# The modulation's weight loads stand in pairs in the load stream of a hybrid decoder layer

## The chip, the cores and the metric

One core of a Trainium2 chip runs the whole kernel. Times are device microseconds of that core; the kernel before took 1602.75 us as the median of three runs (1599.96 to 1604.44). Its profile is one further execution.

## The reference, cut to what matters

One inference step of one decoder layer, for a prompt of 256 tokens and eight sequences with one new token each, with the same weights. The conditioning vectors `c` (1 + 8 rows) give the modulation; the rest of the layer needs it at two places.

```python
mod = silu(c) @ w_mod + b_mod                    # (9, 2048) @ (2048, 6144)
shift, scale, gate = split(mod, 3)
h = rmsnorm(x, g_pre) * (1 + scale) + shift      # needed by every product with w_in
(u, v, z, xb, zb, q, k, v, qi, ki, wi, zc, gm) = split(h @ w_in)
...                                              # three branches: gMLP, RG-LRU, sparse attention
o = merged @ w_out
y = x + gate * rmsnorm(o, g_post)                # gate is needed at the end only
```

All of it is float32.

## The kernel before, in words

**Weights.** All 264 columns (256 prompt tokens and 8 samples) stay in SBUF; the weights stream past. A weight tile (a "w item") is one load of 512 KB from `in_wall`: eight blocks of 128x128. ScalarE rounds it to a high part (`wh`, L157 through `split_high`), VectorE makes the low part (`wl`, L160 through `split_low`), in two halves of 512 columns each, and TensorE multiplies each block three times (high x high, high x low, low x high: L1008 in `product`). So a w item is 24 products of 264 columns in fp32r. There are 482 of them, numbered from 0 in the order of the stream.

**Modulation.** An "m item" is one load of 512 KB from `in_wmod`, which TensorE reads as it is, in fp32, with the conditioning (`cpad`, padded to 32 columns) as the stationary operand (L394 in `mod_item`). The result of each takes only 32 columns of the array, and up to four groups lie side by side in the tile `pmod`: the profile shows these products with a tile of 128*32, those of L1008 with 128*128. An item of 1024 columns is 4 products, 8 in the profile, since it shows two for each fp32 product. There are 96 m items. The hidden state is built in six pieces of 1, 1, 2, 4, 4, 4 blocks of 128 features (`PIECES`); piece q needs the items m q.0, m q.1 and so on: 4, 4, 8, 16, 16 and 16 of them. The last 32, m 6.x and m 7.x, make the gate.

**The order of the work** is a list, `STREAM`, written out by `_stream` (L75 to L98) before anything is emitted. It sets the order of the loads on SP's queue, of the splits and of the products alike. It begins with the 4 items of piece 0. Then come the first 32 output blocks (`EARLY`), one piece of features at a time: the w items of piece q, with the m items of piece q + 1 between them, each as soon as its due position has come (`MOD_BY`, L83). That is 4, 4, 8, 16, 16 and 16 w items, w0 to w63. Then come the other blocks whole, two w items each; in the part of `u` and `za` (the gMLP branch) one gate item follows every w item until the 32 gate items are used up (L90 to L95).

**Buffers.** Loads land in ten buffers, six called `raw` and four called `rawx`; after the last item of piece 5 only the six are left (`room`, L243). They are taken from a list in the order in which they were given back (`load`, L248; `used`, L259). An m item gives its buffer back when TensorE has read it; a w item when VectorE has made the second half of `wl`. A load waits on SP until its buffer is free, and every load behind it waits with it. The split tiles `wh` and `wl` have three buffers each (`AHEAD + 1`): a tile is split two tiles ahead of its products in the main part, one ahead at the beginning (`split_plan`, L270). The work of ScalarE and VectorE is emitted in the order of the list too: a split that stands before the evacuations of a tile (`part`, L159 and L1014) holds them up while it waits.

**Index keys.** When the last item of piece 5 has been emitted, `gather_kix` (L473) puts 32 small loads (L483) on SP's queue. They come behind the weight loads that had been emitted by then, and ahead of all the others.

```python
    for i, it in enumerate(items):
        while room(loaded):
            load(loaded); loaded += 1
        ...
            split_plan(); split_some(...)
        if it[0] == "m":
            mod_item(i); continue
        ...                                  # a w item: product() for its blocks
```

Of the kernel before, what the change touches and what calls it, by code (L numbers as in the profile page):

```python
# [36 lines left out]
ORDER = [("ki", 0)]  # L37
# [37 lines left out]
def _stream():  # L75


    items, n = [("m", 0, i) for i in range(len(MODS[0]))], 0
    for q, (k0, nk) in enumerate(PIECES):
        ms = [("m", q + 1, i) for i in range(len(MODS[q + 1]))] if q + 1 < len(PIECES) else []  # L80
        done = 0
        for j in range(0, EARLY, 8 // nk):
            while done < len(ms) and done * MOD_BY <= j * len(ms):  # L83
                items.append(ms[done])
                done += 1
            items.append(("w", n, [(x, k0, nk) for x in range(j, j + 8 // nk)]))
            n += 1
        assert done == len(ms)
    gate = [("m", q, i) for q in range(len(PIECES), len(MODS)) for i in range(len(MODS[q]))]
    for j in range(EARLY, len(ORDER)):  # L90
        for k0 in (0, 8):
            items.append(("w", n, [(j, k0, 8)]))
            n += 1
            if gate and ORDER[j][0] in ("u", "za"):
                items.append(gate.pop(0))  # L95
    return items


STREAM = _stream()


# [1084 lines left out]
```

## Time and profile before

| | us |
|---|---|
| median of three runs | 1602.75 (1599.96 to 1604.44) |
| the profiled execution, its own time | 1604.95 |
| its span, first to last instruction | 1603.2 |
| TensorE busy | 1572.6 |
| VectorE busy | 987.1 |
| ScalarE busy | 808.1 |
| mean granted TensorE clock | 0.993 |

The span runs from the first to the last instruction of the core. Busy products overlap, so the distance between the starts of two products is what one costs, not its own duration. In the rows PE is TensorE's product, PEld its weight load, DVE VectorE, ACT ScalarE, POOL GpSimd, SPq the queue of SyncE. L394 means line 394 of the kernel. An entry in brackets gives the idle time of the engine just before the row and what ended it.

### The profile page before, as it was taken

The page shows a single profiled execution, that of the slowest core. Times are in us where ns is not written, and L with a number is a line of the kernel's source. Part 1 is how long each engine was busy: PE and PEld are TensorE (multiplying, and loading weights), DVE is VectorE, ACT ScalarE, POOL GpSimd, SP SyncE. Part 2 cuts the span into 40 slices and gives each one's busy share as a digit, 9 for nine tenths or more (in the row PEclk, how much of TensorE's full clock was granted, in tenths as well). Part 3 has the DMA queues.
Part 4 walks back from the last instruction along what each step waited for, and adds up shares of the span by engine and source line. Part 5 has one row for each costly group of instructions (what it writes and reads, how often), then busy time and mean ns, then how long its engine had stood idle before and what let it go on. Part 6 is the DMA issues. An engine that isn't in the chain of part 4 may idle for free.

```text
span 1603.2 us, 33544 instructions
## 1 busy us (share of the span) xinstructions
PE 1572.6 (98%) x13353; PEld 1517.7 (95%) x13353; DVE 987.1 (62%) x2100; ACT 808.1 (50%) x1628; POOL 148.0 (9%) x255
## 2 busy tenths in 40 slices
PE   8999979999999999999999999999999999999998
PEld 7888878999999999998889999999999999999998
DVE  6776558865566546444456654444777777766554
ACT  5333337755555444443334444444777777744442
POOL 4000007300000001000000000000211211100011
PEclk9999989999999999999999999999999999999999
DMA  8898753666555656557875556555455555555652
GB/s 337 306 344 290 272 186 114 197 211 195 158 172 170 197 179 197 187 190 265 285 278 174 177 185 228 185 184 180 156 192 172 172 169 187 172 190 185 236 182 84
DMA packets 99773, 326.28 MB, mean 204 GB/s; under 512 B 11552, under 2 KB 23200, under 8 KB 99232
## 3 DMA queue, kind: packets, MB, share of 16 engines
q1 hardware_dynamic: 98816, 322.98, 59.7%
q8 instruction: 105, 1.72, 0.4%
q10 hardware_dynamic: 800, 1.15, 0.2%
q14 instruction: 52, 0.43, 0.1%
HBM read 320.35 MB, written 3.67 MB: 202 GB/s over the span
## 4 chain that ended last, share of the span: by engine, by line
PE 91%; DVE 3%; DMA 2%; ACT 1%; SPq 1%; issue 1%; DVEq 0%; ACTq 0%
PE acc L1008 85%; PE pmod L394 2%; DMA raw<-in_wall 2%; DVE wl L160 1%; SPq L483 1%; ACT wh L157 1%; PE spP L836 0%; PE sP L668 0%; PE oP L680 0%; DMA xr<-in_xT 0%; PE giP L877 0%; PE gaP L877 0%; DVE part L159 0%; PE soP L744 0%; PE ssP L718 0%
## 5 line engine op out<-in xcount | busy, mean ns | idle before, releaser
L160 DVE TENSOR_TENSOR wl<-raw,wh 128x512 fp32r<-128x512 f32 x926 | 612.6, 706 | 387.3 <-ACT wh L157 380.2
L1008 PE MATMUL acc<-hh,wh 128*128 128x264 f32 x2832 | 822.1, 290 | 7.4 <-DVE part L159 3.3
L1008 PE MATMUL acc<-hh,wl 128*128 128x264 f32 x2832 | 805.1, 284 | 1.9 <-DVE wl L160 1.9
L1008 PE MATMUL acc<-hl,wh 128*128 128x264 f32 x2832 | 805.8, 285 | 0.1
L157 ACT ACTIVATE wh<-raw 128x512 fp32r<-128x512 f32 x926 | 530.3, 622 | 498.7 <-PE acc L1008 319.8
L1008 PEld LDWEIGHTS acc<-hh,wh 128*128 128x128 f32 x2832 | 536.1, 189 | 39.4 <-issue 26.1
L1008 PEld LDWEIGHTS acc<-hl,wh 128*128 128x128 f32 x2832 | 536.6, 189 | 0.7 <-DVE hl L160 0.4
L1008 PEld LDWEIGHTS acc<-hh,wl 128*128 128x128 f32 x2832 | 534.0, 189 | 2.3 <-DVE wl L160 2.3
L1008 PE MATMUL acc<-ah,wh 128*128 128x264 f32 x768 | 217.9, 284 | 0.0
L1008 PE MATMUL acc<-al,wh 128*128 128x264 f32 x768 | 217.6, 283 | 0.0
L1008 PE MATMUL acc<-ah,wl 128*128 128x264 f32 x768 | 217.5, 283 | 0.0
L1008 PEld LDWEIGHTS acc<-al,wh 128*128 128x128 f32 x768 | 144.8, 188 | 0.0
L1008 PEld LDWEIGHTS acc<-ah,wh 128*128 128x128 f32 x768 | 144.7, 188 | 0.0
L1008 PEld LDWEIGHTS acc<-ah,wl 128*128 128x128 f32 x768 | 144.0, 187 | 0.0
L159 DVE TENSOR_TENSOR part<-acc,part 128x264 f32<-128x264 f32 x128 | 51.8, 427 | 37.6 <-PE acc L1008 37.2
L1008 PE MATMUL acc<-mh,wh 128*128 128x264 f32 x256 | 72.6, 284 | 0.0
L1008 PE MATMUL acc<-ml,wh 128*128 128x264 f32 x256 | 72.5, 283 | 0.0
L1008 PE MATMUL acc<-mh,wl 128*128 128x264 f32 x256 | 72.5, 283 | 0.0
L808 POOL TENSOR_TENSOR mg<-mg,gp 128x264 f32<-128x264 f32 x16 | 12.1, 753 | 473.3 <-DMA raw<-in_wall 310.7
L1008 PEld LDWEIGHTS acc<-ml,wh 128*128 128x128 f32 x256 | 48.2, 188 | 0.0
L1008 PEld LDWEIGHTS acc<-mh,wh 128*128 128x128 f32 x256 | 48.2, 188 | 0.0
L1008 PEld LDWEIGHTS acc<-mh,wl 128*128 128x128 f32 x256 | 48.0, 187 | 0.0
(362 smaller groups left out, 1142.2 us busy)
## 6 DMA issues: line engine op xcount, KB each, us to landing
raw<-in_wall SPq DMA_DIRECT2D x463, 512.0 KB, 3.6
raw<-in_wmod SPq DMA_DIRECT2D x73, 512.0 KB, 4.7
rawx<-in_wmod SPq DMA_DIRECT2D x23, 512.0 KB, 6.2
rawx<-in_wall SPq DMA_DIRECT2D x19, 512.0 KB, 5.6
gk<-in_ck SPq DMA_DIRECT2D x32, 128.0 KB, 3.5
gv<-in_cv SPq DMA_DIRECT2D x32, 128.0 KB, 4.1
xr<-in_xT SPq DMA_DIRECT2D x4, 528.0 KB, 6.3
wrg<-in_wrg SPq DMA_DIRECT2D x1, 2048.0 KB, 9.9
```

The costliest lines, as they stand in the source:

```text
L157: copy = lambda out, x, scale=1.0: act.activation(out, x, AF.Copy, scale=scale)
L159: add = lambda out, x, y: dve.tensor_tensor(out, x, y, OP.add)
L160: sub = lambda out, x, y: dve.tensor_tensor(out, x, y, OP.subtract)
L394: pe.matmul(MOD[q][32 * g:32 * g + 32, 0:n], cpad[:, k, :], r[:, c:c + n], start=k == 0, stop=k == KB - 1, skip_group_check=True)
L483: sp.dma_start(kix[h:h + 64, b, g * P:(g + 1) * P], a["cidx"][bass.ds(S["pages"][i] * 64, 64), :])
L808: pool.tensor_tensor(S["mg"][:, j, :], S["mg"][:, j, :], x, OP.add)
L1008: pe.matmul(c[:, 0:T], x[:, kk * P:(kk + 1) * P], y[:, k, :], start=n == 0 and (kk == 0 if early else k == 0), stop=n == 2 and (kk == nk - ...
```

## The change

Two loops of `_stream` put m items into the list two at a time. In the early part, when the next m item is due, it and the one after it are appended together. In the part of `u` and `za`, two gate items follow the second w item of a block instead of one following each. Number, content and mutual order of the m items stay; so do those of the w items. What else follows, follows from the new order: which buffer a load gets, and what stands ahead of it in each queue.

```diff
@@ _stream, early part @@
             while done < len(ms) and done * MOD_BY <= j * len(ms):
-                items.append(ms[done])
-                done += 1
+                items += ms[done:done + 2]
+                done += 2
             items.append(("w", n, [(x, k0, nk) for x in range(j, j + 8 // nk)]))
             n += 1
@@ _stream, the other blocks @@
         for k0 in (0, 8):
             items.append(("w", n, [(j, k0, 8)]))
             n += 1
-            if gate and ORDER[j][0] in ("u", "za"):
-                items.append(gate.pop(0))
+        if gate and ORDER[j][0] in ("u", "za"):
+            items += gate[:2]
+            del gate[:2]
```

The list between w7 and w15, before and after (an m item as piece.number):

```
before  3.0 w8 3.1 3.2 w9 3.3 3.4 3.5 w10 3.6 3.7 3.8 w11 3.9 3.10 3.11 w12 3.12 3.13 3.14 w13 3.15 w14 w15
after   3.0 3.1 w8 3.2 3.3 w9 3.4 3.5 w10 3.6 3.7 3.8 3.9 w11 3.10 3.11 w12 3.12 3.13 3.14 3.15 w13 w14 w15
```

At the very beginning it was `0.0 0.1 0.2 0.3 1.0 w0 1.1 w1 1.2 w2 1.3 w3` and becomes `0.0 0.1 0.2 0.3 1.0 1.1 w0 w1 1.2 1.3 w2 w3`.

## Rows read from the trace of the kernel before

**Rows 1.** The page, part 1: busy us, share of the span, instructions

```profile
PE 1572.6 (98%) x13353; PEld 1517.7 (95%) x13353; DVE 987.1 (62%) x2100; ACT 808.1 (50%) x1628; POOL 148.0 (9%) x255
```

**Rows 2.** The page, part 4: the chain of waits by line

```profile
PE acc L1008 85%; PE pmod L394 2%; DMA raw<-in_wall 2%; DVE wl L160 1%; SPq L483 1%; ACT wh L157 1%; PE spP L836 0%; PE sP L668 0%; PE oP L680 0%; DMA xr<-in_xT 0%; PE giP L877 0%; PE gaP L877 0%; DVE part L159 0%; PE soP L744 0%; PE ssP L718 0%
```

**Rows 3.** Stretch of the gates: length, busy PE PEld DVE ACT POOL, clock, DMA share, GB/s

```profile
714.60:832.06 117.46, 117.46 (x1028) 100.44 (x1027) 57.23 (x109) 44.34 (x86) 0.00 (x0) 1.00 0.79 276
```

**Rows 4.** Timeline of PE around one gate item: start us, us, what

```profile
714.48 0.28 PE L1008 MATMUL acc<-hl,wh 128*128 128x264 f32 x1
714.60 0.28 PE L1008 MATMUL acc<-hh,wl 128*128 128x264 f32 x1
714.81 0.64 PE L394 MATMUL pmod<-raw,cpad 128*32 128x256 f32 x8
...
715.61 0.28 PE L1008 MATMUL acc<-hl,wh 128*128 128x264 f32 x1
```

**Rows 5.** Timeline of PE around two m items in a row, piece 4

```profile
109.28 0.28 PE L1008 MATMUL acc<-hh,wl 128*128 128x264 f32 x1
109.49 0.64 PE L394 MATMUL pmod<-rawx,cpad 128*32 128x256 f32 x8
109.95 0.61 PE L394 MATMUL pmod<-raw,cpad 128*32 128x256 f32 x8
...
110.72 0.29 PE L1008 MATMUL acc<-hl,wh 128*128 128x264 f32 x1
```

**Rows 6.** Timeline of ACT and of DVE: one split in the gates

```profile
734.09 1.15 ACT L157 ACTIVATE wh<-raw 128x512 fp32r<-128x512 f32 x2 [2.72 <-DMA raw<-in_wall]
...
734.75 1.29 DVE L160 TENSOR_TENSOR wl<-raw,wh 128x512 fp32r<-128x512 f32 x2 [2.58 <-ACT wh L157]
```

**Rows 7.** The page, part 6: loads, KB each, median us from issue to landing

```profile
raw<-in_wall SPq DMA_DIRECT2D x463, 512.0 KB, 3.6
```

**Rows 8.** Timeline of SP's queue: the index-key loads: start us, us, what

```profile
199.07 22.36 SPq L483 DMA_DIRECT2D kix<-in_cidx  x32
```

**Rows 9.** Timeline of SP's queue: the issues of w11, w12 and w13

```profile
65.19 0.42 SPq L257 DMA_DIRECT2D raw<-in_wall  x1
...
72.65 0.33 SPq L257 DMA_DIRECT2D raw<-in_wall  x1
...
79.85 0.33 SPq L257 DMA_DIRECT2D raw<-in_wall  x1
```

**Rows 10.** Timeline of SP's queue: the issues of w0 and of m1.1

```profile
9.36 0.33 SPq L257 DMA_DIRECT2D raw<-in_wall  x1
10.66 0.33 SPq L255 DMA_DIRECT2D rawx<-in_wmod  x1
```

**Rows 11.** Timeline of ACT: the split of w0

```profile
19.77 1.15 ACT L157 ACTIVATE wh<-raw 128x512 fp32r<-128x512 f32 x2 [1.57 <-DMA raw<-in_wall]
```

**Rows 12.** Timeline of ACT: the splits of w11, w12 and w13

```profile
70.67 1.16 ACT L157 ACTIVATE wh<-raw 128x512 fp32r<-128x512 f32 x2 [4.76 <-PE pmod L394]
77.87 1.15 ACT L157 ACTIVATE wh<-raw 128x512 fp32r<-128x512 f32 x2 [6.05 <-DMA raw<-in_wall]
84.48 1.15 ACT L157 ACTIVATE wh<-raw 128x512 fp32r<-128x512 f32 x2 [5.45 <-DMA raw<-in_wall]
```

**Rows 13.** Timeline of PE: the first product of w13, and the item behind it

```profile
86.92 0.36 PE L1008 MATMUL acc<-hh,wh 128*128 128x264 f32 x1 [1.89 <-DVE part L159]
...
91.52 0.64 PE L394 MATMUL pmod<-raw,cpad 128*32 128x256 f32 x8
```

**Rows 14.** Stretch after PE's wait at w13, columns as in rows 3

```profile
88.00:90.00 2.00, 2.00 (x12) 2.00 (x11) 1.67 (x4) 1.32 (x3) 0.00 (x0) 0.52 0.96 377
```

**Rows 15.** Second half of the opening, columns as in rows 3

```profile
60.00:98.36 38.36, 35.59 (x331) 29.65 (x329) 26.02 (x67) 12.73 (x26) 0.00 (x0) 0.96 0.93 351
```

**Rows 16.** DMA, 0 to 100 us: what the engines moved in 40 equal slices

```profile
GB/s 30 177 355 412 412 404 406 410 405 406 407 410 367 244 208 329 187 318 69 347 167 410 264 313 408 418 310 360 365 259 362 357 211 377 288 331 379 405 415 410
```

## The prediction, made before the changed kernel was run

> **What bounds the kernel now.** The busy times come first: PE is busy 1572.6 of 1603.2 us [rows 1]. A busy PE alone proves little, so the chain of waits is read next: 85% of it is the trunk's product (L1008), 2% the modulation's product (L394), and 1% each is work that PE waits for, among it the loads of the index keys on SP's queue, L483 [rows 2]. Then the stretches: from 714.60 to 832.06, where the 32 gate loads are consumed, PE is busy for the whole 117.46 us at full clock [rows 3]. There every nanosecond saved on PE is saved at the end. Only two places are not PE's, and the sum takes them up: the opening up to about 92 us, where weights and their splitting come late, and the loads of the index keys.
>
> **The count.** The change is said to halve 96 changes of tile width to 48. Walking the list by its rule says otherwise, since neighbours already shared a visit. Runs of m items before, then after: head with piece 1, 4 then 2; piece 2, 4 then 4; piece 3, 7 then 6; pieces 4 and 5, 12 then 8 each; gates, 32 then 16. That is 71 then 44: 27 visits go, not 48.
>
> **The price of one visit.** PE's timeline shows one m item alone: the last product of a weight tile starts at 714.60, the second product after the item at 715.61, 1.01 us [rows 4]. I count to the second product because the first after an item is slow as well. Two plain steps of 0.12 (714.48 to 714.60) would have taken 0.24, so a lone item costs 0.77. With two items in a row the same distance is 109.28 to 110.72, 1.44 us, less 0.24: 1.20 [rows 5]. The second item costs 0.43. A merged visit therefore saves 0.77 - 0.43 = **0.34 us**; as both kinds run in the kernel of before, this price needs no guess.
>
> **The sum, part by part.**
> - Gates: 16 merges in a stretch where PE never idles [rows 3]: 16 x 0.34 = -5.4 us. All of it reaches the end if loads keep up. After the change every other weight load goes into a buffer that the splitting of the tile two ahead sets free. That splitting takes 1.95 us (ACT from 734.09, DVE to 736.04) [rows 6]. From there four tiles of 24 x 0.12 = 2.9 us and two pairs of 1.2, less the 1.95 already gone, leave 12.0 us before the product, 10.0 before the tile's own splitting must begin. A load takes 3.6 [rows 7]. Covered.
> - Pieces 4 and 5: 8 merges, but the last of them (the end of piece 5) lies after the point from which the index-key loads are timed, so its 0.34 is lost in that wait: 7 x 0.34 = -2.4.
> - Index-key loads: SP works in order. They start at 199.07 and hold the queue for 22.36 us before the next weights [rows 8]. Before, two weight loads stand behind the last splitting that frees a buffer ahead of them; after, only one does, the other having got its buffer from PE earlier. One issue of 0.42 [rows 9] fewer: -0.4. Gathering is called one tile earlier, but with one more tile already loaded, so PE runs dry at the same tile.
> - The start pays. Loads go out in stream order, and m1.1 now stands before tile 0. Tile 0's load is issued at 9.36, the next at 10.66 [rows 10]; ACT sat waiting for it until 19.77 [rows 11]. One place later is **+1.3**. The bounds are 0, if later waits of this stage swallow it, and +3, if PE's longer idling also brings a further stretch at half clock, priced below. I take 1.3, which the two rows give.
> - The wait at tile 13 goes. Tiles 11, 12 and 13 use one buffer in turn, so each load waits for the splitting of the tile before: issued at 65.19, 72.65, 79.85 [rows 9], while ACT gets them at 70.67, 77.87 and 84.48 [rows 12]. PE then idles 1.89 us before 86.92, and the tile that begins there takes 4.6 us to the next item (91.52) instead of 2.9 [rows 13]: the granted clock is 0.52 in that stretch, the lower level of 1.2 GHz, after that idling [rows 14]. By the changed list tile 12 gets the buffer of m3.3, which PE frees before tile 9, and goes out behind the splitting of tile 10, not 11. What limits it then is the queue, which in the full opening issues a load per 1.3 us [rows 10]: tile 11, behind one more m item, lands near 71.9, then m3.10, m3.11 and tile 12 at 75.8, 2.0 sooner than 77.87. Its splitting (1.95) ends near 77.8; m3.15 and tile 13 go out behind it, at 78.3; with the same 4.6 to landing (79.85 to 84.48) tile 13 is there at 82.9 and split at 84.9. PE arrives at 85.0 as before plus one item of 0.43, so it no longer waits and does not idle its clock away: 1.9 and 1.7, **-3.6**. Bounds: 0, if landing takes longer as loads come sooner, and -4.
> - Nothing else is added: instructions, bytes and loads are the same, and the m items move earlier, so what they compute is ready no later.
>
> Sum: -5.4 - 2.4 - 0.4 + 1.3 - 3.6 = -10.5 us. The profiled execution took 1604.95 (span 1603.2 and 1.75 around it), which gives 1594.45. It lies 2.2 above the median of the runs, 1602.75; against that the forecast is 1602.75 - 10.5 = 1592.25, rounded **1592.5**.
>
> **Rivals.**
> - *The opening is bound by bytes.* From 60 to 98.36 us the queue moved 351 GB/s, its share 0.93 [rows 15]; if that is the ceiling, no order of loads brings tile 13 sooner, the wait stays, and the start's 1.3 may stay too: -5.4 - 2.4 - 0.4 + 1.3 = -6.9, or 1595.9. Against it: the same queue moved 404 to 412 GB/s over several slices between 7.5 and 30 us, and later fell as low as 69 [rows 16]. There is room. The Trainium skill (DMA: Bandwidth & Descriptors, Specifications) limits one core's HBM reads to about 358 GB/s, which would make this rival the likeliest. By that rule the trace disagrees with its 412. Chance 0.22.
> - *It does what it says.* 48 visits vanish: 48 x 0.34 = -16.3, or 1586.4. The walk of the list speaks against it; it could come near only if the opening also gained more than I see. Chance 0.05.
> - *No change.* PE reaches its tiles sooner and waits there for loads, so the gates give nothing: -2.4 - 0.4 + 1.3 is -1.5, or 1601.3. For it: in bursts a pair asks for three loads at once. Against it: the 12.0 us of lead. Chance 0.12.
> - *Slower: loads late at the gates.* With pairs, two buffers of six hold m tiles at the same time, and every other weight load starts only after a splitting. It decides once a load takes over 10.0 us instead of 3.6. To lose 4.8 net after gaining 10.5, 16 such tiles must each be late by 15.3 / 16 = 0.96 us, so loads would take about 11 us: 1607.6. The gate stretch runs its DMA at 0.79 share and 276 GB/s [rows 3], far from the 412 that this queue has shown. Chance 0.06.
>
> **How the numbers follow.** The forecast has 0.55. Its own spread is the opening's terms and the clock after the index-key loads, where PE restarts at half clock for a stretch whose end may shift by a couple of us. The range, 1586 to 1600, holds these, the rival of bytes and the one of 48; no change and slower (0.18 together) are left out. A measurement of this kernel can tell about 0.3%, 4.8 us, so faster means below 1597.9. Faster is the forecast (0.55), two thirds of the rival of bytes (0.15 of 0.22), whose middle lies only 2 us below that bound, and the one of 48 (0.05): 0.75. Within 0.3% is the rest of the bytes (0.07) and the third rival (0.12): 0.19. Slower 0.06.
>
> **What would show it.** PE's timeline in the gates: pairs with 1.44 us between the products around them, weight tiles of 2.9 us, and no wait named between; the stretch of the gates shorter by 5.4. In the opening: tile 0's load landing near 21, no idle time of PE near 87 us and no granted clock below 1 there. The index-key loads should start near 194 (199.07 + 1.3 - 3.6 - 2.4 - 0.4). Wrong it would be if a pair cost twice 0.77, if ACT in the gates waited for loads with PE idle behind it, or if PE still idled before tile 13.

## The result, and the profile after

The changed kernel takes 1612.89 us, the median of five runs (1610.25 to 1614.11); the kernel before ran five times beside it with a median of 1602.3 (1599.96 to 1604.44). The ratio is 1.0062, with an interval of 1.0051 to 1.0073: about 10 us slower. Forecast were 1592.5 us, with 1586 to 1600 as the range, so even the sign was wrong. The profiled execution took 1614.11 us (span 1612.3). All line numbers behind the edit are one higher than before, and L395, L1009, L158 and L161 are the L394, L1008, L157 and L160 of the rows above.

Parts 1 and 4 of the profile's page of the changed kernel (busy time; the chain that ended last):

```profile
PE 1572.5 (98%) x13353; PEld 1523.6 (94%) x13353; DVE 985.8 (61%) x2100; ACT 806.7 (50%) x1628; POOL 148.4 (9%) x255
...
PE acc L1009 82%; DMA raw<-in_wall 3%; PE pmod L395 2%; DVE wl L161 2%; DMA rawx<-in_wall 1%; SPq L484 1%; ACT wh L158 1%; DVE part L160 1%; DMA xr<-in_xT 0%; PE sP L669 0%; PE oP L681 0%; PE spP L837 0%; PE giP L878 0%; PE gaP L878 0%; PE soP L745 0%
```

The number of instructions is that of [rows 1], and so, to 0.1 us, is PE's busy time. The chain is where the difference shows: the trunk's product fell from 85% to 82% [rows 2], and what came in its place are loads (3% and 1%) and splits. PE waits more, and for weights.

Where along the kernel it does so is read by counting products: 24 of them make a weight tile, so the start of every tile can be found on PE's timeline in both traces. After minus before, in us:

| tile | w0 | w12 | w13 | w16 | w48 | w52 | w192 | w200 | w206 | w210 | w214 | w222 | w230 | w480 |
|---|---|---|---|---|---|---|---|---|---|---|---|---|---|---|
| | +1.25 | -0.01 | +2.19 | +3.18 | -0.04 | -0.54 | -0.73 | -1.74 | -2.75 | -3.30 | -0.77 | +4.79 | +9.16 | +9.20 |

From tile 194 the gate items come. Up to tile 210 each pair brings about its 0.34 us, as forecast (2.57 us in eight). Then, in twenty tiles, more than 12 us are lost, and nothing changes behind. The stretch of the gates, with the same columns as [rows 3], is:

```profile
714.00:841.50 127.50, 117.82 (x1039) 103.29 (x1037) 54.24 (x104) 42.16 (x85) 0.00 (x0) 0.99 0.66 240
```

PE stands still for 9.7 of 127.5 us, where [rows 3] had none, and the DMA moves less per second, 240 GB/s instead of 276. The pair itself costs what it should. PE's timeline around one of them, early in the gates:

```profile
738.65 0.28 PE L1009 MATMUL acc<-hh,wl 128*128 128x264 f32 x1
738.86 1.07 PE L395 MATMUL pmod<-raw,cpad 128*32 128x256 f32 x16
739.86 0.39 PE L1009 MATMUL acc<-hh,wh 128*128 128x264 f32 x1
740.09 0.28 PE L1009 MATMUL acc<-hl,wh 128*128 128x264 f32 x1
```

From 738.65 to 740.09 are 1.44 us, the very figure of [rows 5]. What PE waits for stands on SP's queue, ACT and PE a little later. SP's queue (start, us, what):

```profile
762.01 0.80 SPq L256 DMA_DIRECT2D raw<-in_wmod  x2
762.87 2.59 SPq L258 DMA_DIRECT2D raw<-in_wall  x2
770.17 0.80 SPq L256 DMA_DIRECT2D raw<-in_wmod  x2
771.02 0.90 SPq L258 DMA_DIRECT2D raw<-in_wall  x2
779.63 0.80 SPq L256 DMA_DIRECT2D raw<-in_wmod  x2
780.49 2.58 SPq L258 DMA_DIRECT2D raw<-in_wall  x2
788.03 0.80 SPq L256 DMA_DIRECT2D raw<-in_wmod  x2
```

ACT in the same stretch (in brackets its idle time and what ended it):

```profile
768.18 1.15 ACT L158 ACTIVATE wh<-raw 128x512 fp32r<-128x512 f32 x2 [3.89 <-DMA raw<-in_wall]
...
777.65 1.15 ACT L158 ACTIVATE wh<-raw 128x512 fp32r<-128x512 f32 x2 [7.00 <-DMA raw<-in_wall]
...
786.05 1.15 ACT L158 ACTIVATE wh<-raw 128x512 fp32r<-128x512 f32 x2 [3.87 <-DMA raw<-in_wall]
```

DVE, and PE's first product of the tile (in brackets again the idle time before it):

```profile
778.31 1.29 DVE L161 TENSOR_TENSOR wl<-raw,wh 128x512 fp32r<-128x512 f32 x2 [5.79 <-ACT wh L158]
```

```profile
778.33 0.39 PE L1009 MATMUL acc<-hh,wh 128*128 128x264 f32 x1 [1.91 <-ACT wh L158]
```

Follow one round, from one pair's issue to the next. At 771.02 a weight load goes out, third behind two gate items. ACT has it at 777.65, 6.63 us later, against a median of 3.6 [rows 7]. DVE ends its low parts at about 779.60. That frees the buffer, and at 779.63 SP issues the next two gate items and, behind them, the next weights. Round after round hangs on the one before: the 14 issues of a pair between 718.95 and 833.65 lie 114.70 / 13 = **8.82 us** apart. PE, which gets two tiles and a pair in each round, could do one in about 7.2 (below, `e3_more`), and now idles 1.91 us ahead of the tile.

The waits of the gates, grouped (us in total, times, longest); first the changed kernel:

```profile
ACT wh L158 <- DMA raw<-in_wall: 68.4, 14, 7.4
...
PEld acc L1009 <- ACT wh L158: 11.5, 10, 2.4
```

then the kernel before, in its own stretch of the gates (where PE never idles, [rows 3]):

```profile
ACT wh L157 <- DMA raw<-in_wall: 44.1, 20, 3.9
```

ACT waited for loads before too, but never over 3.9 us and without holding PE up. Now it waits up to 7.4, and PE's weight loads wait for ACT ten times.

**The opening.** SP's queue of the changed kernel, the issues of w0 (with w1), of w12, of m3.12 to m3.15, and of w13:

```profile
10.66 1.61 SPq L258 DMA_DIRECT2D rawx<-in_wall  x2
...
69.06 0.66 SPq L258 DMA_DIRECT2D raw<-in_wall  x1
75.30 4.12 SPq L256 DMA_DIRECT2D raw<-in_wmod  x4
79.46 0.90 SPq L258 DMA_DIRECT2D rawx<-in_wall  x2
```

ACT, the splits of w0, w11, w12 and w13:

```profile
21.02 1.15 ACT L158 ACTIVATE wh<-rawx 128x512 fp32r<-128x512 f32 x2 [2.83 <-DMA rawx<-in_wall]
...
73.31 1.15 ACT L158 ACTIVATE wh<-raw 128x512 fp32r<-128x512 f32 x2 [7.14 <-DMA raw<-in_wall]
77.10 1.15 ACT L158 ACTIVATE wh<-raw 128x512 fp32r<-128x512 f32 x2 [2.63 <-DMA raw<-in_wall]
86.67 2.41 ACT L158 ACTIVATE wh<-rawx 128x512 fp32r<-128x512 f32 x4 [8.41 <-DMA rawx<-in_wall]
```

Two stretches of it, columns as in [rows 3]: from the issue of m3.12 to the landing of w13, and one behind PE's wait:

```profile
75.30:86.70 11.40, 10.38 (x116) 7.60 (x108) 3.98 (x10) 1.19 (x3) 0.00 (x0) 1.00 0.90 338
...
90.00:92.00 2.00, 2.00 (x11) 2.00 (x11) 1.53 (x3) 0.00 (x0) 0.00 (x0) 0.50 0.94 367
```

Tile 0 landed at 21.02, as forecast. Tile 13 did not gain: it was issued a little sooner than in [rows 9] (79.46 for 79.85), but landed at 86.67 instead of 84.48 [rows 12], behind four modulation items. PE stood idle for longer (3.14 us), began the tile at 89.11 (86.92 in [rows 13]) and again went on at half its clock, as in [rows 14].

**The index keys.** SP's queue:

```profile
199.24 21.82 SPq L484 DMA_DIRECT2D kix<-in_cidx  x32
221.15 2.97 SPq L258 DMA_DIRECT2D raw<-in_wall  x6
```

They begin 0.17 us later than in [rows 8], but weights go on 0.38 sooner (221.15; 221.53 before). The forecast had them begin near 194.

### The profile page after: what moved, and what is told of

Same layout as the page of the kernel before. It is cut to its first block, busy times and chain, and to the rows that moved or that the text cites. A ratio compares the mean times of both kernels' runs of the same rounds, so it can differ in the third digit from the quotient of the medians.

```text
span 1612.3 us, 33543 instructions
## 1 busy us (share of the span) xinstructions
PE 1572.5 (98%) x13353; PEld 1523.6 (94%) x13353; DVE 985.8 (61%) x2100; ACT 806.7 (50%) x1628; POOL 148.4 (9%) x255
## 4 chain that ended last, share of the span: by engine, by line
PE 88%; DVE 4%; DMA 4%; SPq 1%; ACT 1%; issue 1%; DVEq 0%; ACTq 0%
PE acc L1009 82%; DMA raw<-in_wall 3%; PE pmod L395 2%; DVE wl L161 2%; DMA rawx<-in_wall 1%; SPq L484 1%; ACT wh L158 1%; DVE part L160 1%; DMA xr<-in_xT 0%; PE sP L669 0%; PE oP L681 0%; PE spP L837 0%; PE giP L878 0%; PE gaP L878 0%; PE soP L745 0%
## 5 line engine op out<-in xcount | busy, mean ns | idle before, releaser
L161 DVE TENSOR_TENSOR wl<-raw,wh 128x512 fp32r<-128x512 f32 x934 | 618.0, 706 | 396.1 <-ACT wh L158 378.9
L1009 PE MATMUL acc<-hh,wh 128*128 128x264 f32 x2832 | 822.6, 290 | 14.5 <-ACT wh L158 10.3
L1009 PE MATMUL acc<-hh,wl 128*128 128x264 f32 x2832 | 807.9, 285 | 3.4 <-DVE wl L161 3.4
L1009 PE MATMUL acc<-hl,wh 128*128 128x264 f32 x2832 | 808.4, 285 | 0.0
L158 ACT ACTIVATE wh<-raw 128x512 fp32r<-128x512 f32 x934 | 535.0, 622 | 519.3 <-PE acc L1009 325.7
L1009 PEld LDWEIGHTS acc<-hh,wh 128*128 128x128 f32 x2832 | 538.6, 190 | 36.6 <-ACT wh L158 22.3
L1009 PEld LDWEIGHTS acc<-hh,wl 128*128 128x128 f32 x2832 | 536.3, 189 | 5.9 <-DVE wl L161 5.9
L1009 PEld LDWEIGHTS acc<-hl,wh 128*128 128x128 f32 x2832 | 538.8, 190 | 0.6 <-DVE hl L161 0.2
L1009 PE MATMUL acc<-ah,wh 128*128 128x264 f32 x768 | 218.0, 284 | 0.0
L1009 PE MATMUL acc<-al,wh 128*128 128x264 f32 x768 | 217.7, 283 | 0.0
L1009 PE MATMUL acc<-ah,wl 128*128 128x264 f32 x768 | 217.5, 283 | 0.0
L1009 PEld LDWEIGHTS acc<-al,wh 128*128 128x128 f32 x768 | 144.8, 189 | 0.0
L1009 PEld LDWEIGHTS acc<-ah,wh 128*128 128x128 f32 x768 | 144.7, 188 | 0.0
L1009 PEld LDWEIGHTS acc<-ah,wl 128*128 128x128 f32 x768 | 144.0, 188 | 0.0
L160 DVE TENSOR_TENSOR part<-acc,part 128x264 f32<-128x264 f32 x128 | 51.7, 430 | 35.3 <-PE acc L1009 35.2
L1009 PE MATMUL acc<-mh,wh 128*128 128x264 f32 x256 | 72.7, 284 | 0.0
L1009 PE MATMUL acc<-ml,wh 128*128 128x264 f32 x256 | 72.6, 283 | 0.0
L1009 PE MATMUL acc<-mh,wl 128*128 128x264 f32 x256 | 72.5, 283 | 0.0
L1009 PEld LDWEIGHTS acc<-ml,wh 128*128 128x128 f32 x256 | 48.3, 188 | 0.0
L1009 PEld LDWEIGHTS acc<-mh,wh 128*128 128x128 f32 x256 | 48.2, 188 | 0.0
L1009 PEld LDWEIGHTS acc<-mh,wl 128*128 128x128 f32 x256 | 48.0, 188 | 0.0
```

What stands on the lines that cost most here:

```text
L158: copy = lambda out, x, scale=1.0: act.activation(out, x, AF.Copy, scale=scale)
L160: add = lambda out, x, y: dve.tensor_tensor(out, x, y, OP.add)
L161: sub = lambda out, x, y: dve.tensor_tensor(out, x, y, OP.subtract)
L1009: pe.matmul(c[:, 0:T], x[:, kk * P:(kk + 1) * P], y[:, k, :], start=n == 0 and (kk == 0 if early else k == 0), stop=n == 2 and (kk == nk - ...
```

## The experiments

Four theories of the loss were held against each other. **A, the loop:** loads, splits and the freeing of six buffers form a closed round, and pairs make it longer than PE's. **B:** the opening shifts the cost to the gates. **C:** the queue can't move the bytes of the gates fast enough. **D:** the splits of two tiles, now back to back, come late for PE. Diffs are against the changed kernel where a part is undone, else against the one named. The kernel before ran beside all of them: 1602.29 us (19 runs) with the first four, 1602.66 (13 runs) with the others.

### Each half of the change alone

`e1_early` undoes the gates:

```diff
-        if gate and ORDER[j][0] in ("u", "za"):
-            items += gate[:2]
-            del gate[:2]
+            if gate and ORDER[j][0] in ("u", "za"):
+                items.append(gate.pop(0))
```

> Only the early part of the list has its m items in pairs; the gates stand alone as before. Theory A (the loss sits in the gates: the paired gate loads wait for a splitting, a weight load goes out third in the burst behind them, and the round of load, landing and splitting is longer than PE's two tiles and a pair): PE's start of tile 152 some 0.5 us sooner than before, as in the changed kernel, and nothing lost after it, 1601.7 in all. Rival B (the new order of the opening shifts something that is paid later, so the gates lose whatever their order is): about 1612. In the opening both expect tile 13 later by about 2 us, as in the changed kernel.

Measured: 1601.43 us (11 runs), ratio 0.9999 [0.9991, 1.0008].

`e2_gates` undoes the early part:

```diff
-                items += ms[done:done + 2]
-                done += 2
+                items.append(ms[done])
+                done += 1
```

> Only the gates have their m items in pairs; the early part is as before. Theory A: the whole loss is here, first some 2.4 us sooner over seven pairs, then 12 us lost, 9.7 slower than before, about 1612. Rival B: no loss without the early part, 1602.3 - 5.4 = 1597.

Measured: 1618.25 us (4 runs), ratio 1.0096 [1.0082, 1.0111].

On PE's timeline `e1_early` is 3.65 us ahead of the kernel before at tile 194 and 3.65 ahead at tile 480: nothing is lost in the gates. (The profiled execution of before was 2.2 us over its median, so 3.65 there and a ratio of 1 go together.) Expected at tile 152 was a lead of 0.5, as in the changed kernel; it was 3.48. Of these 3 us, 1.8 arise between tiles 12 and 16, with the same order of loads: PE waited 2.57 us there instead of 3.14, and its clock did not fall:

```profile
88.06 0.36 PE L1008 MATMUL acc<-hh,wh 128*128 128x264 f32 x1 [2.57 <-ACT wh L157]
...
88.00:92.00 4.00, 3.94 (x32) 3.97 (x33) 3.83 (x13) 0.97 (x5) 0.00 (x0) 1.00 0.90 274
```

So two executions of one opening can differ by some 3 us. `e2_gates` is 2.81 ahead at tile 194, 4.49 at tile 204, and 15.48 behind at tile 230. So the gates alone make the loss, with either opening: **B falls**.

Between tiles 194 and 230 `e2_gates` lost 8.4 us more than the changed kernel. Its trace says where. PE's rounds exceed their price from tile 204 on (8.34 us for 7.44), in the changed kernel from tile 210 on; by then 3.9 of the 8.4 are gone, and from tile 210 to 230 it needs 90.0 us where the changed kernel needs 85.5. Its loop is longer: the 14 issues of a pair from 716.87 to 836.30 lie 9.19 us apart, for 8.82, and the third load of these bursts takes 6.20 us to landing on average, for 5.79. Why it lands later is open. The granted clock fell there as well, where PE had idled (0.91 and 0.94 of full; columns as in [rows 3]); that this adds to the loss is not shown.

```profile
780.00:800.00 20.00, 17.40 (x138) 15.46 (x139) 8.79 (x18) 7.05 (x15) 0.00 (x0) 0.91 0.56 212
820.00:850.00 30.00, 27.41 (x229) 24.67 (x229) 12.58 (x24) 8.67 (x18) 0.00 (x0) 0.94 0.68 247
```

### One buffer more

`e3_more` is `e2_gates` with a seventh load buffer, from the middle of the branch before the gates on; in the whole kernel a pool of small work tiles has 10 tiles instead of 12 to make room for it.

```diff
-        return work.tile([P, n], dt, name=name, tag="w", bufs=12)
+        return work.tile([P, n], dt, name=name, tag="w", bufs=10)
...
+        free.extend((ab.tile([P, 8 * P], F32, name=f"rawy{n}"), True) for n in range(1))
```

> The gates in pairs, the early part as before, and one load buffer more from the middle of the third branch on (seven instead of six; to make room the pool of small work tiles has 10 tiles instead of 12 in the whole kernel). Theory A: with seven buffers the first load of a pair goes out one splitting earlier and the weight load is second in its burst instead of third; the round is about as long as PE's 7.0 us, so the waits shrink to 2 us or less and the gates gain 3 to 5.4, 1597 to 1600. Rival C (the queue cannot move the bytes of a burst in the time, whatever the buffers): as with six, about 1612. Rival D (two splittings now stand back to back on ACT and DVE, and their order holds PE up): as with six, about 1612.

Measured: 1596.9 us (5 runs), ratio 0.9967 [0.9955, 0.998]. The gates of `e3_more`:

```profile
712.00:828.00 116.00, 116.00 (x1062) 104.41 (x1061) 58.85 (x113) 44.93 (x89) 0.00 (x0) 1.00 0.75 273
```

PE never idles, and the pairs bring their price: 2.30 us ahead of before at tile 194, 7.62 at tile 230, so 5.32 for 16 pairs. The same bytes in the same order now go at 273 GB/s, against 240, and the splits come in the same order as in `e2_gates`: **C and D fall**, and A stands. From tile 194 to 226, where the 16 pairs stand, PE takes 115.7 us, 7.23 a round, which is its own pace. From tile 210 to 230, eight rounds with a pair and two without, it takes 70.4. The changed kernel's 85.5 are 15.1 more.

### The pairs further apart

`e4_gatesu` is `e2_gates`, but with a pair behind each block of `u` only, so one pair per four tiles:

```diff
-        if gate and ORDER[j][0] in ("u", "za"):
+        if gate and ORDER[j][0] == "u":
```

> The gates in pairs, but a pair only after each u block, so every four weight tiles instead of two, over twice the stretch; the early part is as before. As many merges (16). Theory A: in a round of four tiles and a pair PE has 12.8 us, more than the round of load, landing and splitting, so no waits: 16 x 0.34 = 5.4 us gained, about 1597. Rival D: splittings back to back are the same here, so waits of about 1.7 us a pair remain: 1597 + 16 x 1.7 = 1624 at most, at least no gain. Rival C also expects 1597, since the bytes per time are fewer.

Measured: 1596.42 us (8 runs), ratio 0.9967 [0.9957, 0.9978]. The part in which it consumes its gate items:

```profile
712.00:930.00 218.00, 218.00 (x1909) 206.40 (x1908) 121.60 (x233) 92.02 (x184) 0.00 (x0) 1.00 0.67 237
```

No idle time with six buffers either: between two pairs, a round of plain tiles lets the loads catch up. From tile 194 (1.59 ahead) to tile 258 (7.21) it gains 5.6, by the price 16 x 0.34 = 5.4.

### One buffer fewer, and no pairs

If the loop is what counts, the kernel before must have stood close to its edge. `e6_fewer` is that kernel with one of six buffers put aside while the gates run:

```diff
+    kept = []
+    def fewer():
+        kept.append(free.pop(0))
+    def again():
+        free.append(kept.pop())
-    BEFORE = {("pc", 8): start_a, ("pa", 2): start_b}
+    BEFORE = {("pc", 8): start_a, ("u", 0): fewer, ("u", 8): again, ("pa", 2): start_b}
```

> The kernel of before with its lone gate items, but with five load buffers instead of six from u 0 to u 8, that is while the gate items last. Theory A: now every weight load waits for the splitting of the tile just before it, so each of 32 tiles takes a round of splitting (1.95) and landing (3.6 to 4) and the issue between them, 5.6 to 6 us instead of 3.67: the stretch of the gates grows from 117 us to 180 to 192, about 1665 to 1677 in all. Rival C (bytes) and rival D (order of splittings): nothing of theirs has changed, 1602.

Measured: 1662.62 us (4 runs), ratio 1.0366 [1.035, 1.0382]. Its gates, columns as in [rows 3]:

```profile
714.00:890.00 176.00, 137.62 (x1035) 113.29 (x1027) 53.65 (x103) 42.31 (x83) 0.00 (x0) 0.92 0.49 174
```

Three weight loads on SP's queue there, and the split of the first on ACT:

```profile
745.52 0.33 SPq L257 DMA_DIRECT2D raw<-in_wall  x1
...
751.35 0.33 SPq L257 DMA_DIRECT2D raw<-in_wall  x1
...
757.19 0.33 SPq L257 DMA_DIRECT2D raw<-in_wall  x1
```

```profile
749.37 1.15 ACT L157 ACTIVATE wh<-raw 128x512 fp32r<-128x512 f32 x2 [4.40 <-DMA raw<-in_wall]
```

Here the loop is shortest and plain: issue at 745.52, landing at 749.37 (3.85 us, first in its burst), split 1.95, next issue at 751.35, 5.83 us after the last, for one tile. It cost 60 us, just under what was expected. The same arithmetic, issue, landing and split per round, holds for singles with five buffers and for pairs with six.

### The opening

In piece 3 the pairs put four items ahead of tile 13. `e7_nop3` leaves that piece in single items, keeps the pairs in the others, and has the gates of before:

```diff
+                k = 1 if q == 2 else 2
-                items += ms[done:done + 2]
-                done += 2
+                items += ms[done:done + k]
+                done += k
```

> The early part in pairs except the items of piece 3, which stay in their old places; gates alone as before. Theory A for the opening (tile 13 comes late because the four loads m3.12 to m3.15 go out just ahead of it and it lands only after them): the load of tile 13 lands within 4 to 5.5 us of its issue as before, PE waits before it no more than the 1 to 1.9 us of before, and the pairs of pieces 4 and 5 and the shorter queue before the index keys remain: about 1598. Rival (the later start of tile 0 is what makes tile 13 late): as with all early pairs, 1601.4.

Measured: 1600.34 us (9 runs), ratio 0.9981 [0.9971, 0.9991]. SP's queue, ACT and PE at tile 13 in `e7_nop3`:

```profile
81.33 0.33 SPq L258 DMA_DIRECT2D raw<-in_wall  x1
```

```profile
85.94 1.15 ACT L158 ACTIVATE wh<-raw 128x512 fp32r<-128x512 f32 x2 [5.44 <-DMA raw<-in_wall]
```

```profile
88.38 0.42 PE L1009 MATMUL acc<-hh,wh 128*128 128x264 f32 x1 [2.00 <-DVE part L160]
```

The landing took 4.6 us from the issue, as [rows 9, 12] have it, instead of the 7.2 behind four items. But the issue came at 81.33, so the tile was there at 85.94, and PE waited 2.00 us. The time, 1600.34, lies between the two that were expected. **Inconclusive:** before at 84.48, the changed kernel at 86.67, this one at 85.94. Moreover, the opening of `e7_nop3` ran in three kernels, and tile 16 began 1.90 us later than before in it, 0.79 later in `e8_best` and 1.92 sooner in `e9_quads`. One trace does not settle a term of 2 us here.

### Both together

`e8_best` has the opening of `e7_nop3` and the gates of `e4_gatesu`.

> The early part in pairs except piece 3, and a pair of gates after each u block. Theory A: both gains add, 1598 - 5.4 = 1592.6. If the opening's theory is wrong: 1601.4 - 5.4 = 1596.

Measured: 1593.95 us (5 runs), ratio 0.9942 [0.9928, 0.9955]. That is 6.4 below `e7_nop3`; on PE's timeline 5.6 of it arise between tiles 194 and 258, as in `e4_gatesu`, and add to the opening's part.

`e9_quads` goes a step further: the opening of `e7_nop3`, and four gate items behind every second block of `u`, eight tiles apart (the gates' part of the diff, against the changed kernel).

```diff
-        if gate and ORDER[j][0] in ("u", "za"):
-            items += gate[:2]
-            del gate[:2]
+        if gate and ORDER[j][0] == "u" and ORDER[j][1] % 2 == 0:
+            items += gate[:4]
+            del gate[:4]
```

> As the kernel with a pair after each u block, but four gate items after every second u block: 24 merges instead of 16. If loads keep up: 24 x 0.34 = 8.2 gained in the gates, 1598 - 8.2 = 1590. Theory A warns: the four loads go out ahead of a weight load that waits for a splitting too; a run of eight tiles and four items gives PE 25.2 us, and three weight loads in a row wait each for the splitting two tiles before, 6.7 us a round against PE's 5.8, which the two tiles already split should absorb. So 1590, or up to 1595 if they don't.

Measured: 1591.44 us (5 runs), ratio 0.9922 [0.9909, 0.9936], faster than both kernels. The part in which it consumes its gate items:

```profile
712.00:925.00 213.00, 213.00 (x1889) 204.45 (x1888) 120.46 (x230) 91.03 (x182) 0.00 (x0) 1.00 0.69 240
```

PE is busy throughout. From tile 194 to tile 258 it gains 13.21 - 5.21 = 8.0 us, against 24 merges x 0.34 = 8.2.

## Why the prediction was wrong

By its own terms, with what PE's timeline shows for each (differences of the table above):

| term | forecast | after |
|---|---|---|
| gates (tile 192 to 230) | -5.4 | +9.9 |
| pieces 4 and 5 (tile 16 to 48) | -2.4 | -3.2 |
| index keys (tile 48 to 52) | -0.4 | -0.5 |
| start (tile 0) | +1.3 | +1.25, back to 0 by tile 12 |
| wait at tile 13 (tile 12 to 16) | -3.6 | +3.2 |

The rest of the 9.2, some -1.5, lies between these stretches: -1.26 from tile 0 to 12 and -0.19 from tile 52 to 192.

**Right:** the price of a merged visit and the count. 0.34 us held in every stretch where PE did not idle: 5.3 for 16 in `e3_more`, 5.6 for 16 in `e4_gatesu`, 8.0 for 24 in `e9_quads`. The 16 merges counted in the gates were 16. Pieces 4 and 5 gave somewhat more, -3.2, in all five kernels with these pairs.

**The index keys** came out as to the queue, not as to the size. One weight load instead of two goes out between the last split that frees a buffer and the keys, as forecast. But from the first issue behind that split to the keys it takes 2.12 us (197.12 to 199.24) where it took 2.26 (196.81 to 199.07): 0.14 us less, not 0.42. The -0.5 of the table is no proof of the term, since from their start to the next weights it takes 21.6 to 22.2 us in four further executions with the queue of before, for 22.46 in the one of [rows 8] and 21.91 after.

**The step that failed** is "Covered", behind the gates. "12.0 us before the product, 10.0 before the tile's own splitting must begin. A load takes 3.6" compared a lead with a duration. Two things were wrong in it. The first is the size. 3.6 is the median of all 463 loads; a weight load that goes out third in a burst takes longer, here 6.63 and 5.56 us (771.02 to 777.65, 780.49 to 786.05). The second is the kind, and it weighs more. The lead was counted as if each round found it again. But the next weight load can only be issued when this one has landed and been split, whatever PE does: 0.86 us for the two items issued ahead of it, 5.2 to 6.9 to landing, 1.95 of split. That is 8.0 to 9.7 us a round (the issues measure 8.2 to 9.8), for two tiles and a pair that PE finishes in 7.2. So the lead is a stock on which the loop draws in each round. Counted from the issue of a tile's load on SP to its first product on PE, in us:

| tile | w200 | w202 | w204 | w206 | w208 | w210 | w212 to w226 |
|---|---|---|---|---|---|---|---|
| before | 13.3 | 12.5 | 12.8 | 13.0 | 13.3 | 11.9 | 10.8 to 13.1 |
| after | 12.6 | 11.8 | 10.3 | 8.9 | 6.7 | 6.0 | 6.0 to 7.7 |
| `e3_more` | 13.1 | 12.1 | 10.4 | 10.9 | 10.0 | 10.3 | 8.3 to 10.5 |

(Every second tile; after the change it is the one behind the pair.) At tile 200 the changed kernel has the 12.0 us of the forecast. Its issue and its first product, and the first product of tile 210, whose issue at 762.87 stands above:

```profile
719.81 3.57 SPq L258 DMA_DIRECT2D raw<-in_wall  x2
```

```profile
732.42 0.39 PE L1009 MATMUL acc<-hh,wh 128*128 128x264 f32 x1
...
768.87 0.39 PE L1009 MATMUL acc<-hh,wh 128*128 128x264 f32 x1
```

In the five rounds between, the issues lie 43.06 / 5 = 8.61 us apart and PE's starts 36.45 / 5 = 7.29: each round takes 1.3 us of the lead. At 6.0 us it holds no more than the landing and the first half of the split, and from then on PE went at the loop's pace, ten rounds in 85.5 us where `e3_more` took 70.4. The lead of `e3_more` falls too, by some 0.3 us a round. Its seventh buffer makes the loop nearly as short as PE's round, and lasts for these 16 pairs; that it would last for more is not shown.

The same bookkeeping shows why the kernel before just held. There, too, the split of every second tile gave its buffer to a modulation item, but the weight load came second, behind one item. SP's queue of the kernel before, around the split of [rows 6]:

```profile
729.39 0.33 SPq L257 DMA_DIRECT2D raw<-in_wall  x1
...
736.07 0.33 SPq L255 DMA_DIRECT2D raw<-in_wmod  x1
736.45 0.42 SPq L257 DMA_DIRECT2D raw<-in_wall  x1
```

Issued at 729.39, landed at 734.09 (4.70 us), split by 736.04 [rows 6], next item at 736.07, next weights at 736.45: a round of 7.06 us for two tiles, which with their two single items cost PE 121.03 / 16 = 7.56 (tiles 194 to 226). By this one round it had 0.5 us to spare; over all of them the lead in the table neither grows nor runs down. The change lengthened the loop by the load's place in the burst and shortened PE's side by 0.34. That the edge was near is shown by `e6_fewer`.

**The rival that came true** is "slower: loads late at the gates", which had 0.06 and 1607.6 us. Its mechanism was right, buffer for buffer, but its condition, "it decides once a load takes over 10.0 us", was wrong for the same reason: no weight load in the gates took over 7.6. "No change" had the right question ("a pair asks for three loads at once") and was answered with the lead as well. The DMA's mean share of 0.79 was taken as room. A mean over a stretch says nothing of a loop with gaps in it. The DMA view of the changed kernel, 770 to 800 us in 40 slices of 0.75 us, with the loads issued in it (count, KB, median us to landing):

```profile
GB/s 0 115 224 306 415 410 415 426 388 98 22 0 0 0 164 295 355 415 355 415 426 366 6 0 0 109 180 393 431 426 382 415 382 77 22 0 0 27 218 251
...
raw<-in_wmod SPq DMA_DIRECT2D x8, 512.0 KB, 4.1
raw<-in_wall SPq DMA_DIRECT2D x7, 512.0 KB, 6.5
```

The four loads of a burst move at up to 431 GB/s, then nothing moves for about two microseconds, until a buffer has come free and the next loads have begun. The loop is set by when the burst's weight load lands and is split, not by the mean share.

**The start** was sized right and kept nothing: the 1.25 us were gone at tile 12, so its lower bound of 0 was the better value. **The wait at tile 13** failed in two steps. One is its landing. The issue was forecast for 78.3 and came at 79.46; "the same 4.6 to landing" became 7.2, behind four modulation items. The other is that 1.7 of the 3.6, the price of half clock, was read from one execution. In four further ones with the opening of before (`e2_gates`, `e3_more`, `e4_gatesu`, `e6_fewer`) PE waited 0.99 to 1.73 us at this tile and the granted clock stayed at 1.00, so there was no such 1.7 to win; they pass from tile 12 to 16 in 1.2 to 1.9 us less than the execution of the rows. Against them the changed kernel lost more there than the table's 3.2. The rival "the opening is bound by bytes" said that no order of loads brings tile 13 sooner, and none clearly did. It landed between 83.9 and 84.7 in five executions with the order of before, at 85.5 (`e1_early`) and 86.6 with all pairs, and at 83.5, 84.7 and 85.8 with piece 3 in single items. Whether bytes set that landing is not settled: between 75.30 and 86.70 the share is 0.90, but at 338 GB/s, below the 404 to 412 of [rows 16]. The rival's price (-6.9 in all) was wrong with the gates.

What stays open: why the third load of a burst lands 0.4 us later in `e2_gates` than in the changed kernel, and the opening's share to better than about 2 us.

## What to carry to other kernels

Where loads, their consumer and the freeing of buffers form a ring, don't compare a lead with the duration of a load: add up the ring (issue, landing at its place in the burst, the work that frees the buffer, next issue) and compare it with what the bounding engine needs for the same tiles. If the ring is the longer one, the lead only sets when the loss begins, and a DMA that looks idle on average is no comfort. Merging visits of an engine pays where the ring has time to recover, as with four items every eight tiles here (8.0 us gained in the gates), and turns into a loss where the same merge is packed into every second tile (1.0096).

## What the runs showed of the hardware

- The time from the issue of the same 512 KB load until ACT has it goes with its place in the burst: 3.85 us as the first (`e6_fewer`, 745.52 to 749.37), 5.56 and 6.63 as the third in the gates, 7.21 behind four others in the opening (79.46 to 86.67).
- One core's loads moved up to 431 GB/s in slices of 0.75 us in the gates, and 404 to 412 over nine slices in a row of the opening [rows 16]; a later stretch of the opening had 338. The Trainium skill (DMA: Bandwidth & Descriptors, Specifications) gives about 358 GB/s as the HBM limit of a core, half of the 716 of a stack, divided between two cores. This kernel runs on one core, and its measurement goes above that figure.
- PE's idling of 3.14 us before tile 13 (85.97 to 89.11) was followed by a stretch at the lower of its two clock levels, 0.50 from 90 to 92 us. This does not follow every wait: in `e1_early` the clock stayed at 1.00 behind one of 2.57 us at the same tile, while the kernel before had 0.52 behind one of 1.89 [rows 13, 14]. So what a wait costs in the products behind it can't be read from one execution.
